# A change to the table of durations from which a layer kernel's order of instructions is computed: transfers by row numbers and accumulations

## The chip, the cores and the metric

The kernel runs on one core of one Trainium2 chip. The metric is the time of one execution on the device in microseconds (us). The kernel before the change takes 2641.74 us, the median of three runs from 2641.53 to 2642.2 us. Five engines work beside each other, each through its own list of instructions: PE (matrix products), DVE and ACT (elementwise work), POOL, and SP. SP issues the large transfers, POOL those whose rows are picked by a list of numbers.

## What is computed

One layer over 2048 tokens of width 1024, in fp32: a mixer (four heads of differential attention, four of mLSTM), cross attention to 256 memory rows, a mixture of 32 experts of which each token takes two, and a last norm. The change shows in the experts and in what follows them:

```
x = x + hybrid_mixer(rms_norm(x, norm_mix_g), ...)
x = x + cross_attention(rms_norm(x, norm_x_g), ...)
x = x + hierarchical_moe(rms_norm(x, norm_ffn_g), ...)
return rms_norm(x, norm_final_g)
# hierarchical_moe: a group (of 4), then the 2 best of its 8 experts for each token;
# the rows of each expert are collected into blocks, and
def run_block(args):
    x_blk, e = args
    return (silu(x_blk @ w1[e]) * (x_blk @ w3[e])) @ w2[e]     # w1, w3: 1024 x 512, w2: 512 x 1024
yb = run_block(...) * buf_w                                    # the token's weight for that expert
out = zeros.at[buf_tok].add(yb)                                # added to the rows of the tokens
```

## The kernel before, in words

No engine's order is written by hand. While the kernel's Python runs, every operation is recorded (`Flow.add`, which is line 521 in nearly every row of the profile, so that groups are told apart by their tiles), and `Flow.run` then works out the order of each engine from a model of the program. `Eng.price` is the table of that model: for each operation the time it holds its engine (`cost`), what passes after that until its result is there (`tail`), and for a transfer the bytes that it moves. `forward` plays the program through with these numbers: whenever an engine is free, it takes the ready operation that is most urgent. All transfers share one model of the transfer engines, `ring`, at 360e3 bytes per us, and land 2.0 us (issued by SP) or 2.7 us (POOL) after their bytes are through. `backward` goes through the finished order from its end and gives each operation the latest time at which it could end; from this comes the urgency for the next round. Of ten rounds that with the shortest modelled span is kept. The order so found is fixed in the program: on the chip each engine goes through its list and waits at an instruction until what it needs is there, and what stands behind it waits too.

The stages in time, by the trace: the mixer up to about 1100 us, cross attention up to 1790, the router and the plan of the experts' blocks up to 1880, the experts up to 2580, and the last norm.

An expert goes as follows. `e_in` gathers its rows with an indirect transfer from POOL (`xg`, two buffers), PE turns them over (matmuls of `ident` with `xg`), ACT and DVE split the result into a high and a low part (`xgT`). Its weights, 6 MB, come in six chunks of 1 MB (`eraw`, issued by SP); each chunk is split into two parts as well (`esp`), in halves: twice an ACT CAST for the high part and twice a DVE TENSOR_TENSOR for the low one. PE multiplies with w1 and w3 (`e_w13`, or `e_two` for experts whose rows stand in two blocks, of 64 rows and of the rest; rows of `esp,xgT` and of `xgT,esp`), ACT and DVE make `hT` of that, PE turns it over where needed (`ident,s`) and multiplies with w2 (`e_out`, rows of `esp,hT`). The results leave PSUM into `ys`, by ACT alone, or for blocks of 64 rows by ACT (`lo`) and DVE. `ys` is one buffer for two blocks. Per block one indirect transfer from POOL adds `ys` to the rows of `x2d` in memory (`x2d<-ys,IDX`, an accumulation); these go strictly one behind another, and the first write into `ys` of the next expert waits until those of the expert before have landed.

The experts go through in a fixed order that ends with number 12, 29, 13, 14, 30 and 31 (numbers by rank; 13 and 14 have two blocks, 30 has one of 104 rows and 31 one of 64). The last two, 30 and 31 (`E[-2]`, `E[-1]`), don't use `e_out`: their results are added in the core and written back. `f_load` then reads all of `x2d` in eight transfers of 1 MB (`fx`, four of them into slots of `esp`). They wait for the last accumulation, that of expert 14. ACT takes the squares (`fsq`), DVE multiplies with the norm, SP writes `out_dram`, and at the very end POOL scatters the rows of experts 30 and 31 into it.

Of the kernel before, what the change touches and what calls it, by code (L numbers as in the profile page):

```python
# [187 lines left out]
class Flow:  # L188
# [133 lines left out]
    def backward(self, order, span):  # L322

        import heapq
        free, wait, can, left, ready = {}, {}, {}, {}, {}

        def offer(o):
            heapq.heappush(wait.setdefault(o.eng, []), (ready[o], -o.stop, -o.seq, o))
        for op in order:
            left[op] = sum(1 for o in op.post if o.pre[op] > -5)  # L330
            ready[op] = 0.0
            free[op.eng] = 0.0
            can.setdefault(op.eng, [])
        for op in order:
            if left[op] == 0:
                offer(op)
        for _ in order:
            best = None
            for e in free:
                w = wait.get(e, [])  # L340
                while w and w[0][0] <= free[e] + 0.02:
                    r, p, i, o = heapq.heappop(w)
                    heapq.heappush(can[e], (p, i, o))
                t = free[e] if can[e] else w[0][0] if w else None
                if t is not None and (best is None or t < best[0]):
                    best = (t, e)
            t, e = best
            op = heapq.heappop(can[e])[2] if can[e] else heapq.heappop(wait[e])[3]
            free[e] = op.late = max(t, ready[op]) + op.cost
            for p, lag in op.pre.items():  # L350
                if lag > -5:
                    ready[p] = max(ready[p], op.late + lag + (p.tail if not p.dma else (2.7 if p.eng == "POOL" else 2.0) + p.dma / 360e3))
                    left[p] -= 1
                    if left[p] == 0:
                        offer(p)
        for op in order:
            op.prio = span - op.late

    def forward(self):
# [66 lines left out]
        ring = 0.0  # L426
# [4 lines left out]
        while len(order) < len(self.ops):  # L431
            best = None
            for e in engines:
                while wait[e] and wait[e][0][0] <= free[e] + 0.02:
                    r, p, i, op = heapq.heappop(wait[e])
# [6 lines left out]
            t, e = best  # L442
            if can[e] and e in self.PATIENT:
                p, i, op = can[e][0]
# [4 lines left out]
            op = heapq.heappop(can[e])[2] if can[e] else heapq.heappop(wait[e])[3]  # L449
# [8 lines left out]
            end = op.start + op.cost + op.tail  # L458
            if op.dma:
                ring = max(ring, t) + op.dma / 360e3  # L460
                end = ring + (2.7 if e == "POOL" else 2.0)
            op.stop = end
            for b in op.banks:
                b.lock = (end + self.LINK, e)
# [21 lines left out]
class Eng:  # L486
# [36 lines left out]
    def price(self, fn, out, ins, kw):  # L523
        if "dma" in fn:
            v = out if isinstance(out, View) else kw["in_"]
            return (1.0 if self.eng == "POOL" else 0.45), 0.0, v.cols * (v.p1 - v.p0) * 4
        n = max([v.cols for v in ins] + [out.cols]) if fn not in ("matmul", "transpose") else out.cols
        psum = any(v.tile.whole for v in ins)
        if self.eng == "PE":
# [1590 lines left out]
```

## Time and profile before

| | us |
|---|---|
| time of a run, median of 3 | 2641.74 |
| the profiled execution: its own time | 2654.76 |
| its span in the trace | 2652.9 |
| PE busy in the span | 2526.1 (95%) |
| DVE busy | 1847.3 (70%) |
| ACT busy | 1440.6 (54%) |

The profiled execution is 13.0 us longer than the median of the runs, and its span 1.9 us shorter than its own time. Times in the sections below are places and lengths in this span, counted from its start. The granted clock over the span is 0.982 of full speed.

### The profile page before, as it was taken

Reading aid. Unit: us, or ns where it says so; the run is one execution under the profiler, and the core shown is the slowest. Engines: PE = TensorE matmul, PEld = TensorE weight load, DVE = VectorE, ACT = ScalarE, POOL = GpSimd, SP = SyncE. Lnnn points to the kernel's source line nnn. Section 1 sums busy time; section 2 is a strip of 40 time slices with the busy share of each in tenths; the row PEclk is TensorE's granted clock in tenths of the full one; section 3 lists DMA queues with packets and bytes.
Section 4 is the critical chain, followed back from the end, with each engine's and each line's share of the span. In section 5 each row is a group of like instructions: output and inputs, shape, how many; then the busy total and the mean of one; then the engine's idle time right before and its main releaser. Section 6 shows DMA issues by size and latency. Waiting matters only on the chain. (4 is left out here: it accounts for less than half of the span.)

```text
span 2652.9 us, 43603 instructions
## 1 busy us (share of the span) xinstructions
PE 2526.1 (95%) x15601; PEld 2241.5 (84%) x15601; DVE 1847.3 (70%) x4586; ACT 1440.6 (54%) x2675; POOL 501.4 (19%) x941
## 2 busy tenths in 40 slices
PE   7999999999999999899999999998999999999981
PEld 7999999899999999897888888886888888887871
DVE  5778767777786779876333335668787878887875
ACT  7766555555565555454212223335676667776753
POOL 2322211121122211101110120111321121121220
PEclk9999999999999999999999999999999999999995
DMA  7435333533253327675222255436999999999986
GB/s 244 157 134 145 108 105 94 147 112 103 94 145 114 109 80 240 200 247 199 88 88 89 79 196 196 144 135 220 311 327 306 326 317 328 316 325 299 302 265 253
DMA packets 207853, 509.92 MB, mean 192 GB/s; under 512 B 22807, under 2 KB 104956, under 8 KB 179986
## 3 DMA queue, kind: packets, MB, share of 16 engines
q1 hardware_dynamic: 181896, 395.16, 43.9%
q0 software_dynamic: 22880, 110.20, 14.0%
q8 instruction: 123, 2.02, 0.3%
q10 hardware_dynamic: 2858, 1.75, 0.2%
q14 instruction: 96, 0.79, 0.1%
HBM read 405.97 MB, written 104.76 MB: 193 GB/s over the span
## 5 line engine op out<-in xcount | busy, mean ns | idle before, releaser
L521 DVE TENSOR_TENSOR esp<-eraw,esp 128x1024 fp32r<-128x1024 f32 x384 | 457.4, 1219 | 109.9 <-ACT esp L521 109.3
L521 ACT CAST esp<-eraw 128x1024 fp32r<-128x1024 f32 x384 | 385.2, 1047 | 161.7 <-PE bank L521 83.7
L521 PE MATMUL bank<-xt,wT 128*128 128x256 f32 x3072 | 449.7, 287 | 5.9 <-DMA xt<-xnT 5.2
L521 PEld LDWEIGHTS bank<-xt,wT 128*128 128x128 f32 x3072 | 406.9, 191 | 15.7 <-DMA xt<-xnT 6.0
L521 PE MATMUL bank<-wR,xt 128*128 128x384 f32 (+1 forms) x1536 | 336.8, 347 | 2.2 <-ACT wR L521 2.2
L521 PEld LDWEIGHTS bank<-wR,xt 128*128 128x128 f32 x1536 | 261.3, 190 | 6.0 <-ACT wR L521 2.8
L521 PE MATMUL bank<-esp,hT 128*128 128x512 f32 (+6 forms) x992 | 248.9, 401 | 5.8 <-DVE hT L521 2.2
L521 PE MATMUL bank<-esp,xgT 128*128 128x512 f32 (+3 forms) x944 | 237.9, 401 | 5.8 <-DVE xgT L521 5.6
L521 PE MATMUL bank<-xgT,esp 128*128 128x256 f32 (+7 forms) x1664 | 241.6, 301 | 1.4 <-DVE s L521 1.1
L521 PEld LDWEIGHTS bank<-xgT,esp 128*128 128x128 f32 x1664 | 231.4, 188 | 4.3 <-DVE s L521 1.2
L521 PEld LDWEIGHTS bank<-esp,hT 128*128 128x128 f32 (+6 forms) x992 | 175.7, 181 | 61.3 <-DVE hT L521 4.3
L521 DVE TENSOR_SCALAR_CACHE_REDUCE P<-bank 128x512 f32<-128x512 f32 (+3 forms) x320 | 191.6, 603 | 30.8 <-PE bank L521 29.6
L521 PEld LDWEIGHTS bank<-esp,xgT 128*128 128x128 f32 (+3 forms) x944 | 167.7, 182 | 52.6 <-DVE xgT L521 3.3
L521 ACT ACTIVATE P<-P,zz 128x128 f32<-128x128 f32 (+15 forms) x128 | 154.1, 1204 | 101.7 <-DVE zz L521 100.2
L521 PE MATMUL bank<-VW,pT 128*128 128x512 f32 x768 | 195.1, 400 | 0.0
L521 PE MATMUL bank<-B,xT 128*128 128x512 f32 x768 | 187.1, 395 | 0.0
L521 PE MATMUL bank<-WO,yT 128*128 128x512 f32 x768 | 185.2, 399 | 0.6 <-issue 0.6
L521 PE MATMUL bank<-V,at 128*128 128x256 f32 x1088 | 180.1, 288 | 0.3
L521 PEld LDWEIGHTS bank<-WO,yT 128*128 128x128 f32 x768 | 143.5, 189 | 34.6 <-issue 0.8
L521 PEld LDWEIGHTS bank<-B,xT 128*128 128x128 f32 x768 | 141.8, 188 | 30.5
L521 PEld LDWEIGHTS bank<-VW,pT 128*128 128x128 f32 x768 | 139.8, 188 | 29.6
L521 PEld LDWEIGHTS bank<-V,at 128*128 128x128 f32 x1088 | 151.7, 189 | 2.7 <-ACT bank L521 0.7
(453 smaller groups left out, 4263.7 us busy)
## 6 DMA issues: line engine op xcount, KB each, us to landing
eraw<-in_w_dram SPq DMA_DIRECT2D x192, 1024.0 KB, 8.2
xt<-xnT POOLq DMA_DIRECT2D x64, 1024.0 KB, 6.1
xr<-in_x_dram SPq DMA_DIRECT2D x32, 512.0 KB, 3.7
xnT<-xt SPq DMA_DIRECT2D x16, 1024.0 KB, 3.9
raw<-in_w_in_dram SPq DMA_DIRECT2D x80, 128.0 KB, 2.8
vod<-vo SPq DMA_DIRECT2D x64, 128.5 KB, 3.1
vi<-vod SPq DMA_DIRECT2D x64, 128.5 KB, 2.5
rt<-in_rope_dram SPq DMA_DIRECT2D x32, 256.0 KB, 2.6
```

Of the source, the lines that this page charges most:

```text
L521: flow.add(self.eng, lambda: real(*[bare(a) for a in args], **{k: bare(v) for k, v in kw.items()}), cost, tail, reads, writes, dma)
```

## The change

In the table, an indirect transfer of 512 columns or more (the gathers of `xg`, the accumulations of `ys`, the write-back and the last scatters) gets a tail of 5.0 us where it had none, and a transfer that accumulates counts 7 bytes an element where it counted 4. `forward` and `backward` add the tail of a transfer, which they left out. Nothing that is computed changes, and no line of the kernel's phases does; the instructions of the mixer and of cross attention keep their prices, but all of the program is ordered anew.

```diff
@@ backward @@
-                    ready[p] = max(ready[p], op.late + lag + (p.tail if not p.dma else (2.7 if p.eng == "POOL" else 2.0) + p.dma / 360e3))
+                    ready[p] = max(ready[p], op.late + lag + p.tail + (0.0 if not p.dma else (2.7 if p.eng == "POOL" else 2.0) + p.dma / 360e3))
@@ forward @@
             if op.dma:
                 ring = max(ring, t) + op.dma / 360e3
-                end = ring + (2.7 if e == "POOL" else 2.0)
+                end = ring + (2.7 if e == "POOL" else 2.0) + op.tail
@@ price @@
         if "dma" in fn:
             v = out if isinstance(out, View) else kw["in_"]
-            return (1.0 if self.eng == "POOL" else 0.45), 0.0, v.cols * (v.p1 - v.p0) * 4
+            rows, add = "indirect" in fn and v.cols >= 512, kw.get("compute_op") is not None
+            return (1.0 if self.eng == "POOL" else 0.45), (5.0 if rows else 0.0), v.cols * (v.p1 - v.p0) * (7 if add else 4)
```

What this does to the order is seen in the rows of the two programs. A row is an instruction in an engine's list; the number behind a tile's name tells the tile of one expert or chunk from that of another and is not the same in both programs.

First place, ACT, in the experts shortly before the end, where expert 27's results (`ys_25880` before the change) and those of its follower 28 (`ys_26012`) are written. Before:

```order
L521 ACTIVATE ys_25880<-bank1_80,WS_20630 104x512
L521 CAST hT_25974<-bank1_80 128x4x104
L521 CAST esp_25995<-eraw_25923 128x1024 x2
L521 ACTIVATE ys_26012<-bank7_86,WS_20630 104x512
L521 CAST esp_26018<-eraw_25967 128x1024 x2
L521 CAST esp_26034<-eraw_25893 128x1024 x2
L521 CAST xgT_26062<-bank6_85 128x4x104
L521 CAST xgT_26062<-bank7_86 128x4x104
L521 CAST esp_26072<-eraw_25987 128x1024 x2
L521 ACTIVATE ys_26012<-bank1_80,WS_20630 104x512
```

The same place of the changed program, where the two are `ys_25809` and `ys_26074` of experts 11 and 27; ahead of these rows stand the two writes of `ys_25809` and two casts of `esp_25881`, and behind them the second write of `ys_26074`:

```order
L521 CAST xgT_25819<-bank5_84 128x4x88
L521 CAST esp_25940<-eraw_25879 128x1024 x2
L521 CAST esp_25954<-eraw_25849 128x1024
L521 CAST hT_25967<-bank5_84 128x4x104
L521 CAST esp_25954<-eraw_25849 128x1024
L521 CAST esp_25985<-eraw_25772 128x1024 x2
L521 CAST esp_26004<-eraw_25927 128x1024 x2
L521 CAST xgT_26019<-bank6_85 128x4x104
L521 CAST esp_26039<-eraw_25976 128x1024 x2
L521 CAST xgT_26019<-bank4_83 128x4x104
L521 ACTIVATE s1_26050<-s1_26050 128x304
L521 ACTIVATE ys_26074<-bank7_86,WS_20630 104x512
```

Between the last write of one expert's `ys` and the first of the next stood two casts of weights before (the same holds between expert 11 and 27); now twelve stand there, and the two writes of one `ys` stand side by side. Over all experts the number of such casts went from between 2 and 16 (in two places 2) to between 6 and 18.

Second place, DVE, around the write of expert 14's first block (`ys_26964` before, `ys_27104` after) and the last chunks of weights. Before:

```order
L521 SCALAR_TENSOR_TENSOR ys_26964<-bank0_79,WS_20630,lo_26952 64x512
L521 TENSOR_TENSOR esp_26943<-eraw_26891,esp_26943 128x1024
L521 SCALAR_TENSOR_TENSOR ys_26964<-bank5_84,WS_20630,lo_26973 64x512
L521 TENSOR_TENSOR esp_26943<-eraw_26891,esp_26943 128x1024
L521 TENSOR_TENSOR xgT_26758<-bank1_80,xgT_26758 128x4x104
L521 TENSOR_TENSOR esp_26991<-eraw_26922,esp_26991 128x1024 x2
L521 TENSOR_TENSOR esp_27011<-eraw_26949,esp_27011 128x1024 x2
L521 TENSOR_TENSOR esp_27026<-eraw_26967,esp_27026 128x1024 x2
L521 TENSOR_TENSOR esp_27053<-eraw_26998,esp_27053 128x1024 x2
L521 TENSOR_TENSOR s1_27045<-s1_27045,bank7_86 104x512
L521 TENSOR_TENSOR esp_27077<-eraw_27022,esp_27077 128x1024 x2
L521 TENSOR_TENSOR xgT_27069<-bank0_79,xgT_27069 128x4x64
```

After (a last chunk, `esp_27115`, follows these rows of before; `esp_27113` is the last chunk of after):

```order
L521 TENSOR_TENSOR esp_27007<-eraw_26934,esp_27007 128x1024 x2
L521 TENSOR_TENSOR esp_27024<-eraw_26956,esp_27024 128x1024 x2
L521 TENSOR_TENSOR esp_27043<-eraw_26976,esp_27043 128x1024 x2
L521 TENSOR_TENSOR esp_27057<-eraw_26996,esp_27057 128x1024 x2
L521 TENSOR_TENSOR s1_27071<-s1_27071,bank5_84 104x512
L521 TENSOR_TENSOR esp_27081<-eraw_27031,esp_27081 128x1024 x2
L521 SCALAR_TENSOR_TENSOR ys_27104<-bank0_79,WS_20630,lo_26986 64x512
L521 TENSOR_TENSOR hT_27099<-bank4_83,hT_27099 128x4x104
L521 TENSOR_TENSOR esp_27113<-eraw_27050,esp_27113 128x1024
L521 SCALAR_TENSOR_TENSOR ys_27104<-bank2_81,WS_20630,lo_27120 64x512
L521 TENSOR_TENSOR esp_27113<-eraw_27050,esp_27113 128x1024
L521 TENSOR_TENSOR lo_27136<-bank3_82,lo_27136 64x512
```

Before, fourteen of these splits of weights stood behind the first write of expert 14's `ys`; now two do. On ACT the writes of `ys_27104` stand likewise behind `hT_27099` of expert 30 and ahead of `esp_27113`.

Third place, PE, from the end of expert 14's product with w2 (`hT2_26857` before, `hT2_26926` after) to experts 30 and 31. Before:

```order
L521 MATMUL bank2_81<-esp_26739,hT2_26857 80x512 x7
L521 MATMUL bank7_86<-esp_26864,xgT_26758 104x512 x3
L521 MATMUL bank6_85<-esp_26832,xgT_26758 104x512 x12
L521 MATMUL bank7_86<-esp_26864,xgT_26758 104x512 x9
L521 MATMUL bank7_86<-esp_26903,xgT_26758 104x512 x12
L521 MATMUL bank0_79<-ident_64,xg_26589 128x64 x4
L521 MATMUL bank5_84<-ident_64,xg_26589 128x64 x4
L521 MATMUL bank4_83<-ind_20610,cap_20611 1x32
L521 MATMUL bank3_82<-ident_64,s1_27045 128x104 x4
L521 MATMUL bank1_80<-esp_26917,xgT_27069 128x512 x8
L521 MATMUL bank6_85<-esp_26943,hT_27092 104x512 x12
L521 MATMUL bank7_86<-esp_26991,hT_27092 104x512 x12
```

Behind these rows before stand 24 matmuls of expert 31 with w1 and w3, its `ident,s`, and its 16 with w2. After:

```order
L521 MATMUL bank6_85<-esp_26771,hT2_26926 80x512 x12
L521 MATMUL bank4_83<-esp_26825,xgT_26863 104x512 x12
L521 MATMUL bank5_84<-esp_26876,xgT_26863 104x512 x12
L521 MATMUL bank3_82<-esp_26919,xgT_26944 128x512 x8
L521 MATMUL bank3_82<-esp_27024,xgT_26944 128x512 x8
L521 MATMUL bank7_86<-esp_27043,xgT_26944 128x512 x3
L521 MATMUL bank4_83<-ident_64,s1_27071 128x104 x4
L521 MATMUL bank7_86<-esp_27043,xgT_26944 128x512 x5
L521 MATMUL bank7_86<-esp_27057,xgT_26944 128x512 x8
L521 MATMUL bank5_84<-esp_26947,hT_27099 104x512 x12
L521 MATMUL bank1_80<-esp_27007,hT_27099 104x512 x12
L521 MATMUL bank6_85<-ident_64,s1_27150 128x64 x4
```

Twelve of expert 30's 36 late matmuls and the eight `ident,xg` of expert 31 moved ahead of expert 14's product; expert 31's products with w1 and w3 moved ahead of expert 30's with w2. In the after program the squares (`fsq`) then stand on ACT with no expert's work among them, where before `lo` and `hT` of expert 31 stood between the first eight.

## Rows read from the trace of the kernel before

**Rows 1.** The stages from the plan on, as windows: from:to, length, busy time (and instructions) of PE, of its weight loads, of DVE, ACT and POOL, then PE's granted clock, the busy share of the transfer engines, GB/s.

```profile
1790.00:1880.00 90.00, 81.36 (x401) 64.36 (x400) 73.62 (x234) 51.61 (x62) 20.81 (x17) 0.92 0.67 229
1880.00:2420.00 540.00, 536.05 (x2984) 455.30 (x2983) 445.22 (x542) 378.98 (x504) 114.92 (x71) 1.00 0.98 323
2420.00:2470.00 50.00, 43.48 (x257) 35.17 (x257) 32.95 (x40) 28.91 (x40) 13.88 (x7) 1.00 0.88 273
2470.00:2580.00 110.00, 102.62 (x584) 83.16 (x583) 88.39 (x117) 73.07 (x103) 28.27 (x11) 0.97 0.89 285
```

**Rows 2.** PE's waits between 2420 and 2470 us: what waited for whom, us in total, times, the longest.

```profile
PE bank L521 <- ACT ys L521: 3.6, 2, 1.9
PE bank L521 <- DMA xg<-xn2d,IDX: 1.8, 1, 1.8
PE bank L521 <- DVE s L521: 1.1, 1, 1.1
```

**Rows 3.** ACT in the order of time, two writes of `ys` in that window: start, length, what, and in brackets how long ACT had been idle before it and what ended that.

```profile
2439.27 0.69 ACT L521 ACTIVATE ys<-bank,WS 104x512 f32<-104x512 f32 x1 [5.07 <-issue]
...
2457.15 0.69 ACT L521 ACTIVATE ys<-bank,WS 104x512 f32<-104x512 f32 x1 [4.98 <-DMA x2d<-ys,IDX]
```

**Rows 4.** Transfers between 1880 and 2605 us by tile, from issue to landing: first the gathers `xg`, then the accumulations from `ys`.

```profile
DMA to landing us min/median/max: 5.0/8.7/13.3
```

```profile
DMA to landing us min/median/max: 5.0/9.9/13.9
```

**Rows 5.** POOL in the order of time: the accumulations of experts 13 (two) and 14 (two), and the last scatter into `out_dram`.

```profile
2535.27 3.65 POOL L521 DMA_INDIRECT x2d<-ys,IDX  x1 [17.23 <-DVE ys L521]
2547.32 2.29 POOL L521 DMA_INDIRECT x2d<-ys,IDX  x1 [8.40 <-ACT esp L521]
2561.02 7.18 POOL L521 DMA_INDIRECT x2d<-ys,IDX  x1 [11.41 <-DVE ys L521]
2575.65 1.44 POOL L521 DMA_INDIRECT x2d<-ys,IDX  x1 [7.45 <-DMA x2d<-ys,IDX]
...
2640.08 0.91 POOL L521 DMA_INDIRECT out_dram<-ys,IO  x1 [3.99 <-DMA out_dram<-ys,IO]
```

**Rows 6.** SP's transfers in the order of time: the last seven chunks of weights, then the first reads of `x2d` for the norm.

```profile
2545.26 22.07 SPq L521 DMA_DIRECT2D eraw<-in_w_dram  x7
2580.74 1.40 SPq L521 DMA_DIRECT2D fx<-x2d  x3
```

**Rows 7.** PE in the order of time from the end of expert 14's product with w2 on.

```profile
2549.88 8.52 PE L521 MATMUL bank<-esp,hT 128*80 128x512 f32 x36
2558.23 1.32 PE L521 MATMUL bank<-esp,xgT 128*104 128x512 f32 x5
2562.43 8.80 PE L521 MATMUL bank<-esp,xgT 128*104 128x512 f32 x31 [2.87 <-DVE xgT L521]
2571.16 0.71 PE L521 MATMUL bank<-ident,xg 64*128 64x64 f32 x8
...
2572.97 0.55 PE L521 MATMUL bank<-ident,s 104*128 104x104 f32 x4 [0.97 <-DVE s L521]
2576.22 3.42 PE L521 MATMUL bank<-esp,xgT 128*128 128x512 f32 x8 [2.70 <-DVE xgT L521]
2579.48 5.69 PE L521 MATMUL bank<-esp,hT 128*104 128x512 f32 x24
2585.01 5.77 PE L521 MATMUL bank<-esp,xgT 128*128 128x512 f32 x24
2598.01 0.69 PE L521 MATMUL bank<-ident,s 64*128 64x64 f32 x4 [7.22 <-DVE s L521]
2599.66 5.51 PE L521 MATMUL bank<-esp,hT 128*128 128x512 f32 x16 [0.96 <-DVE hT L521]
```

**Rows 8.** DVE and then ACT in the order of time where expert 14's `ys` is written, with a half chunk of weights and the `hT` of expert 30 on ACT.

```profile
2558.20 0.74 DVE L521 SCALAR_TENSOR_TENSOR ys<-bank,WS,lo 64x512 f32<-64x512 f32 x1 [4.72 <-DMA x2d<-ys,IDX]
...
2560.00 0.74 DVE L521 SCALAR_TENSOR_TENSOR ys<-bank,WS,lo 64x512 f32<-64x512 f32 x1
```

```profile
2559.04 0.69 ACT L521 ACTIVATE lo<-bank,WH 64x512 f32<-64x512 f32 x1 [5.57 <-DVE ys L521]
2559.75 0.68 ACT L521 ACTIVATE ys<-bank,WS 80x512 f32<-80x512 f32 x1
2560.33 1.03 ACT L521 CAST esp<-eraw 128x1024 fp32r<-128x1024 f32 x1
...
2574.20 0.51 ACT L521 CAST hT<-bank 128x416 fp32r<-128x416 f32 x1
```

**Rows 9.** The last norm, the transfer of its input (issues in the window from 2560 us on: KB each, median us to landing), ACT's first square and what stands ahead of it, DVE's longest wait among the multiplications and its last ones.

```profile
fx<-x2d SPq DMA_DIRECT2D x4, 1024.0 KB, 10.4
```

```profile
2593.20 0.63 ACT L521 ACTIVATE s<-lo 64x512 f32<-64x512 f32 x1 [5.47 <-DVE lo L521]
2593.73 1.04 ACT L521 ACTIVATE fsq<-fx 128x1024 bf16<-128x1024 f32 x1
```

```profile
2613.50 0.17 DVE L521 TENSOR_SCALAR rm_h<-fss 128x4 f32<-128x4 f32 x1 [2.41 <-ACT fsq L521]
...
2627.74 2.48 DVE L521 SCALAR_TENSOR_TENSOR esp<-esp,rm_s,gn 128x1024 f32<-128x1024 f32 x2
```

**Rows 10.** The tiles turned over by PE for the experts (all `ident,xg` matmuls after 1880 us): count, then shortest, median and longest in ns, and the first and last start.

```profile
L521 PE MATMUL bank<-ident,xg x344: 221/253/328, 1884.3 to 2571.6; 64*128 64x64 f32 x56, 128*128 128x128 f32 x24, 120*128 120x120 f32 x24, 112*128 112x112 f32 x24
```

## The prediction

> **What bounds the kernel now.** I read the windows by stage first, since the share over the span hides the ends. From 1880 to 2420 us PE is busy for 536.05 of 540 us and the transfer engines for 0.98 of the time [rows 1]. Two resources are full there at once; an order can gain 4 us at most in this stage, and could lose if it only opened a hole. From 2420 to 2470 PE is busy for 43.48 of 50 us, and from 2470 to 2580 for 102.62 of 110: together 13.9 us of idle PE. So I looked at what ends PE's waits in the first of these holes: ACT's writes of `ys` twice, 3.6 us, then a gather, 1.8, then 1.1, in sum 6.5 [rows 2]. Next, why ACT was late: in the order of time it stands idle for 5.07 and 4.98 us in front of just two writes of `ys` [rows 3]. The second is named as a wait for an accumulation `x2d<-ys` to land. The first is put down to nothing that the profile shows; since it stands at the same place of the next expert, I take it for the same wait. These are the two places where the order has only two casts between the `ys` of two experts. Then the landing times: a gather takes 8.7 us in the median (5.0 to 13.3), an accumulation 9.9 (5.0 to 13.9) [rows 4].
>
> The end is a chain of its own. Expert 14's first accumulation is issued at 2561.02 and its second only at 2575.65, once the first is down [rows 5]; 5.09 us later, at 2580.74, SP issues the reads of `x2d` for the norm [rows 6]. I call that moment T0. From there to the span's end at 2652.9 it is 72.2 us, in which PE bounds nothing. So two numbers make the time: T0, and what follows it.
>
> **The change, part by part.** No instruction is added or removed in the phases; only the order moves. For a block of 104 rows (104 x 4 KB = 426 KB) the old table lets a transfer from POOL land after 2.7 + 1.2 = 3.9 us; the new one says 8.9 for a gather and 2.7 + 2.1 + 5.0 = 9.8 for an accumulation. Against 8.7 and 9.9 in [rows 4] the new numbers fit the median, the old ones are less than half.
>
> In sentences that the rest can do without: the Trainium skill, page "DMA: Bandwidth & Descriptors", section "Anatomy of one DMA — SWDGE (gpsimd) path", gives a fit for a transfer from POOL of about 2.0 us plus its bytes at 436 GB/s, so an estimate of 3.0 us for 426 KB. By it the old table would be right and the new one wait for nothing. The trace disagrees: not even the fastest accumulation was below 5.0 us [rows 4]. By the page's figure expert 14's two accumulations would land in some 2.7 us each, and the sum below would come out 5 us lower.
>
> *Waits of ACT at `ys`.* In the new order at least six casts stand between the `ys` of two experts, twelve at the place that now has two. At about 1.03 us a cast [rows 8], twelve cover 12 us, more than the 9.9 of an accumulation. Six cover only 6, but the old order also has sixes and shows no stall of PE at them: all waits of PE in the 540 us before come to 4 us. I credit all 6.5 us of [rows 2]. Bounds: nothing, if DVE or a late chunk of weights ends the wait instead, and 13.9, all the idle PE of both holes.
>
> *Expert 14's accumulations.* This part speaks against the change. Before, expert 14's product with w2 ends on PE at 2549.88 + 8.52 = 2558.4 [rows 7], and its `ys` follows at once: DVE's second write ends at 2560.74 [rows 8]. The new order puts 12 of expert 30's late matmuls and eight transposes ahead of that product: 12/36 x (1.32 + 8.80) = 3.4, and 0.7 [rows 7]. Behind the product, ACT's writes of `ys` stand in line behind `hT_27099`, which needs expert 30's `ident,s`, and ahead of that PE has 24 matmuls of expert 30 (24/36 x 10.12 = 6.7), 19 of expert 31's 32 (19/32 x (3.42 + 5.77) = 5.5) and the `ident,s` itself (0.55): 12.8. So PE gets there at 2558.4 + 4.1 + 12.8 - 6.5 = 2568.8. From there ACT needs `hT` 0.5, two writes of `ys` 1.4, half a chunk 1.0 and `lo` 0.7, then DVE writes for 0.7 [rows 8]: 4.3, so 2573.1, against 2560.74.
>
> What is gained is the landing. Before, the first accumulation took 14.6 us until the second could go, with weights still streaming to 2567 [rows 5, 6]; the second, with the stream over, took 5.09. In the new order both fall behind the stream. For the first I take 5.5 us, near the floor of 5.0 (upper bound 9.9), and 0.7 for POOL to get the second out (it holds POOL for 1.44 [rows 5]). T0 = 2573.1 + 0.3 + 5.5 + 0.7 + 5.1 = 2584.7, 4.0 later than before. The recovered 6.5 us are in this already: without the late accumulations T0 would be earlier by that. Bounds: PE free of the rest of its holes and 5.0 us, T0 -1; nothing recovered in the first hole and 9.9 us, T0 +11.
>
> *The norm.* Before, the first square waits at 2593.73 for a `lo` of expert 31, with ACT idle for 5.47 us ahead [rows 9], 13.0 us after T0; the reads land 10.4 us after their issue. Now no expert's work stands among the squares. That gives 2.6 us at the start. DVE idles 2.41 us among the multiplications for a square that `lo` held up [rows 9]; of that I take a small part, 0.4, since the reads (1 MB each) then press from behind. In sum -3.0; bounds 0 and -5. PE is no obstacle: after `ident,s` at 2568.8 it has 13/32 x 9.19 + 5.69 + 0.69 + 5.51 = 15.6 us left and ends near 2587 even with 2 us of waits, while the first `fx` lands at T0 + 10.4 = 2595. The old wait of 7.2 us for `s` [rows 7] goes too, and gives nothing, since nobody on the path waits for it.
>
> *The plan.* The first expert's gather is now taken to land 5 us later, and its eight transposes (0.253 us each, 2.0 in sum [rows 10]) stand right ahead of its first product. PE idles for 8.6 us in that stage [rows 1]; partly this moves work out of a hole. +1, bounds 0 and +3.
>
> *Mixer and cross attention.* Prices there are unchanged, the order is another one anyway. PE is nearly full there in both programs' lists; I can't price single rows and take 0, bounds -4 and +4, by what the full stage 1880 to 2420 shows as loss of a good order, 4 us.
>
> Sum: +4.0 - 3.0 + 1 + 0 = +2.0 on the span of 2652.9. The profiled execution's own time, 2654.76, goes to 2656.8; it stands 13.0 above the median, so the median of the runs goes from 2641.74 to about 2643.7. I predict 2643.5. The measurement can tell about 0.2%, 5.3 us, from no change.
>
> **The rivals.**
>
> *Faster.* The stalls go and T0 comes early: PE reaches `ident,s` with no hole left (another 4 us of the 13.9), both accumulations land in 5 us. T0 then is 2580, the norm gives its full 5 us, and the shuffle of the mixer some more: 2641.7 - 1 - 5 - 2 = about 2634. For it: the new prices fit the trace at the median, and the waits in [rows 2, 3] are of just the kind that they forbid. Against it: behind 14's `ys` only two splits of weights are left of fourteen, so what is gained in front is spent at the end.
>
> *Slower.* Expert 14's accumulations still fall into the stream: its last chunk is late, since the old order keeps the transfer engines at 0.89 here [rows 1], the first takes 9.9 us, and the second is behind it. T0 + 9 to + 11, the norm -3, the plan +2: about 2651. It decides from the point where the first accumulation takes over 9 us. For it: before, the same one held the next back for 14.6 us while the last chunks streamed. Against it: in the new order at most the last chunk is under way.
>
> *Nothing moves.* Both resources are full from 1880 to 2420, the hole of 6.5 us only shifts what waits for the last chunks, and T0 follows the stream's end: 2641.7 within 2.
>
> **How the numbers follow.** My sum of parts 0.30, nothing moves 0.12, faster 0.26, slower 0.32. The first two lie within 0.2% mostly: same 0.42. The range leaves out about one in ten on each side: 2630 (beyond the 2634 of the faster case, with the mixer's -4) to 2656 (the slower case with the mixer's +4). Alone, my own sum runs from 2639 to 2648.
>
> **What would show it.** In the profile after: ACT without waits of 5 us ahead of `ys` around 2430 to 2460, and PE's busy time there above 48 of 50 us; expert 14's first accumulation issued at about 2573, landing in 5 to 7 us; the reads `fx` at about 2585; the first square 10 to 11 us after them, and 69 us from `fx` to the end. I am wrong if PE's waits for `ys` stay or turn up elsewhere in the experts, if the accumulations of expert 14 take 9 us and more with the stream over, or if the mixer, where no price changed, moves by more than 4 us.

## The result: 1.1% slower

The changed kernel takes 2672.54 us, the median of four runs (2669.53 to 2676.58), against 2641.97 us of the kernel before. The ratio is 1.0112, with a 95% interval from 1.0099 to 1.0125. I had forecast no change, 2643.5 us, with a range up to 2656; the measured time lies 16.5 us beyond it.

The profiled execution took 2669.53 us, its span is 2667.7. The stages in windows, to be held against [rows 1] (from:to, length, busy time of PE, PEld, DVE, ACT and POOL, granted clock, share of the transfer engines, GB/s):

```profile
1790.00:1880.00 90.00, 80.01 (x392) 62.15 (x391) 70.59 (x219) 51.27 (x63) 21.53 (x17) 0.92 0.71 239
1880.00:2420.00 540.00, 523.35 (x2883) 445.49 (x2882) 427.82 (x512) 362.78 (x479) 113.69 (x67) 0.98 0.95 307
2420.00:2470.00 50.00, 48.63 (x252) 37.23 (x252) 36.85 (x44) 33.09 (x46) 11.75 (x6) 1.00 0.92 296
2470.00:2580.00 110.00, 110.00 (x657) 91.37 (x656) 94.82 (x124) 78.67 (x110) 17.95 (x12) 1.00 0.96 320
```

The holes that I had read between 2420 and 2580 us are gone: PE is busy for 158.63 of 160 us there, against 146.10 before. But the stage ahead, which was full, now loses 16.65 of 540 us where it lost 3.95, and its granted clock falls to 0.98. What PE waits for there, the two largest (what waited for whom, us in total, times, the longest):

```profile
PE bank L521 <- DVE xgT L521: 13.2, 6, 3.6
PE bank L521 <- ACT esp L521: 1.1, 1, 1.1
```

One of these places, on PE, ACT and DVE in the order of time (start, length, what, idle before and what ended it):

```profile
2169.86 0.57 PE L521 MATMUL bank<-ident,xg 120*128 120x120 f32 x4
2171.78 0.63 PE L521 MATMUL bank<-ident,xg 120*128 120x120 f32 x4 [1.34 <-DVE xgT L521]
2174.99 6.70 PE L521 MATMUL bank<-esp,hT 128*112 128x512 f32 x17 [2.58 <-DVE xgT L521]
```

```profile
2167.58 2.00 ACT L521 CAST esp<-eraw 128x1024 fp32r<-128x1024 f32 x2 [1.76 <-DMA eraw<-in_w_dram]
2170.47 0.56 ACT L521 CAST xgT<-bank 128x480 fp32r<-128x480 f32 x1 [0.90 <-PE bank L521]
2170.93 1.99 ACT L521 CAST esp<-eraw 128x1024 fp32r<-128x1024 f32 x2
2172.82 0.56 ACT L521 CAST xgT<-bank 128x480 fp32r<-128x480 f32 x1
```

```profile
2171.06 0.66 DVE L521 TENSOR_TENSOR xgT<-bank,xgT 128x480 fp32r<-128x480 f32 x1
2172.01 2.36 DVE L521 TENSOR_TENSOR esp<-eraw,esp 128x1024 fp32r<-128x1024 f32 x2 [0.29 <-ACT esp L521]
2174.28 0.65 DVE L521 TENSOR_TENSOR xgT<-bank,xgT 128x480 fp32r<-128x480 f32 x1
```

PE's list has both groups of `ident,xg` directly ahead of the product with w2, with nothing between. The second `xgT` stands behind a chunk of weights on ACT (2170.93 to 2172.92) and on DVE (2172.01 to 2174.37). So PE waits until DVE empties the bank. It then takes 6.70 us for 17 matmuls, 394 ns each, where a full stretch takes 236 (43 in 10.14 us, below). The same happens at 2226 and 2390. The windows of 20 us around the three places have the clock at 0.84, 0.83 and 0.83, a mean of the two levels:

```profile
2160.00:2180.00 20.00, 16.07 (x79) 13.19 (x78) 15.39 (x17) 12.84 (x17) 4.14 (x2) 0.84 1.01 319
2220.00:2240.00 20.00, 15.91 (x70) 12.60 (x69) 11.54 (x13) 10.59 (x13) 3.92 (x3) 0.83 0.80 249
2380.00:2400.00 20.00, 14.77 (x77) 11.85 (x75) 10.05 (x11) 7.32 (x9) 2.60 (x2) 0.83 0.97 302
```

The end answers to [rows 5 to 9]. PE, POOL, SP and ACT:

```profile
2574.53 10.14 PE L521 MATMUL bank<-esp,xgT 128*104 128x512 f32 x43
2584.51 0.52 PE L521 MATMUL bank<-ident,s 104*128 104x104 f32 x4
```

```profile
2589.86 2.17 POOL L521 DMA_INDIRECT x2d<-ys,IDX  x1 [24.75 <-DVE ys L521]
2596.17 1.43 POOL L521 DMA_INDIRECT x2d<-ys,IDX  x1 [4.14 <-DMA x2d<-ys,IDX]
```

```profile
1788.11 2.23 SPq L521 DMA_DIRECT2D eraw<-in_w_dram  x4
...
2542.21 36.37 SPq L521 DMA_DIRECT2D eraw<-in_w_dram  x11
2601.22 2.46 SPq L521 DMA_DIRECT2D fx<-x2d  x4
```

```profile
2606.90 1.06 ACT L521 ACTIVATE fsq<-fx 128x1024 bf16<-128x1024 f32 x1 [8.01 <-DMA fx<-x2d]
```

T0, the start of the reads for the norm, is 2601.22 instead of 2580.74, and from there to the end it takes 66.5 us instead of 72.2. That is +20.5 - 5.7 = +14.8, the difference of the two spans. The medians lie 30.6 us apart. The other 15.8 belong to the two profiled executions: that of before took 12.8 us more than its median, that of the changed kernel 3.0 us less. The first experiment is about the 12.8.

How PE fares as a whole shows between the first chunk of weights (the first `eraw` of SP's queue, 1793.24 before and 1788.11 now) and the end of PE's last product. The row of that chunk before, the last product now (before, it ends at 2599.66 + 5.51 = 2605.17 [rows 7]), and the two stretches as windows, first before, then now:

```profile
1793.24 2.13 SPq L521 DMA_DIRECT2D eraw<-in_w_dram  x4
```

```profile
2595.52 5.54 PE L521 MATMUL bank<-esp,hT 128*128 128x512 f32 x16 [0.92 <-DVE hT L521]
```

```profile
1793.24:2605.17 811.93, 777.26 (x4268) 647.87 (x4266) 649.54 (x941) 544.32 (x726) 178.42 (x107) 0.98 0.93 306
1788.11:2601.06 812.95, 783.47 (x4268) 652.37 (x4267) 644.02 (x914) 538.13 (x712) 169.71 (x106) 0.98 0.91 295
```

PE's work takes 1.0 us longer: PE idles 5.2 us less (29.5 for 34.7), and the same matmuls take 6.2 us more. What moved is T0 against that work. It lay 24.4 us ahead of the end of PE's last product, so that the norm began beside PE's last work; now it lies 0.2 us behind it.

### The profile page after: what moved, and what is told of

Its sections match the earlier page's. It is cut to its first block, busy times and chain, and to the rows that moved or that the text cites. A ratio compares the mean times of both kernels' runs of the same rounds, so it can differ in the third digit from the quotient of the medians.

```text
span 2667.7 us, 43596 instructions
## 1 busy us (share of the span) xinstructions
PE 2534.3 (95%) x15601; PEld 2247.1 (84%) x15601; DVE 1849.0 (69%) x4586; ACT 1438.9 (54%) x2675; POOL 492.8 (18%) x941
## 5 line engine op out<-in xcount | busy, mean ns | idle before, releaser
L521 PEld LDWEIGHTS bank<-xt,wT 128*128 128x128 f32 x3072 | 406.7, 191 | 12.6 <-DMA xt<-xnT 3.9
L521 PE MATMUL bank<-esp,hT 128*128 128x512 f32 (+6 forms) x992 | 257.7, 410 | 11.0 <-DVE xgT L521 6.6
```

Of the source, the lines that this page charges most:

```text
L521: flow.add(self.eng, lambda: real(*[bare(a) for a in args], **{k: bare(v) for k, v in kw.items()}), cost, tail, reads, writes, dma)
```

## The experiments

All times of the experiments are medians; each ratio is against runs of the kernel before beside it. For the stage in question I use a length that two rows give: from the first chunk of weights (SP's first `eraw`) to T0. It is 2601.22 - 1788.11 = 813.1 us in the changed kernel and 787.5 before.

**The kernel before, profiled again** (no edit).

> The kernel before, unchanged, with a new profile. Its profiled execution of before took 13.0 us more than the median of its runs, and had 6.5 us of idle PE between 2420 and 2470 us and 7.4 between 2470 and 2580. Theory A (the holes belong to the order): the new profile shows them again at the same two writes of ys, and its time stands as far above the runs as before. Theory B (the holes were what that one execution had too much): the new trace, at about 2642 to 2645 us, has PE at 48 of 50 us and more between 2420 and 2470, and about 10 us less idle PE from 1880 to 2580; then the 6.5 us that the prediction credited were not there to be gained.

Measured: ratio 1.0004 (0.9987 to 1.0020); this profiled execution has a span of 2639.4 us. Its window, PE's first wait in it, and SP's rows:

```profile
2420.00:2470.00 50.00, 44.88 (x273) 36.89 (x273) 34.86 (x44) 29.31 (x41) 12.55 (x8) 1.00 0.93 290
```

```profile
PE bank L521 <- ACT ys L521: 3.5, 2, 1.8
```

```profile
1781.49 2.15 SPq L521 DMA_DIRECT2D eraw<-in_w_dram  x4
...
2541.46 15.82 SPq L521 DMA_DIRECT2D eraw<-in_w_dram  x6
2567.34 1.40 SPq L521 DMA_DIRECT2D fx<-x2d  x3
```

The holes are there again (theory A): they belong to the order. Yet the time does not stand 13 us above the runs. The first profile's excess lies elsewhere: its first chunk came at 1793.2 (the first `eraw` of its SP queue), 11.7 us later than here, with the same program. Everything from there to T0 is as long in both, 787.5 and 785.9 us, and so is the rest, 72.2 and 72.1. Against this profile the changed kernel is 28.3 us longer: 6.6 up to the first chunk (where the same program moves by 11.7 from one execution to another), 27.3 from there to T0, and -5.6 behind it. Split by PE's last product, 2.7 of the 27.3 us are PE's work (810.3 us here) and 24.6 the place of T0 against its end. Split by SP's queue, 12.6 lie behind the last chunk's issue: 2601.22 - (2542.21 + 36.37) = 22.6, against 2567.34 - (2541.46 + 15.82) = 10.1.

**Which of the three numbers.** The change has three parts: the 7 bytes, the tail of the gathers and the tail of the accumulations. They were run in five combinations; the accumulations' tail of 5.0 us by itself is not among them. The line that returns the price, in place of the changed kernel's, for both tails, the bytes alone, the gathers' tail alone, the bytes with the accumulations' tail, and the bytes with the gathers' tail (`...` stands for what stays the same):

```diff
-  (5.0 if rows else 0.0), ... * (7 if add else 4)
+  (5.0 if rows else 0.0), ... * 4
+  0.0, ... * (7 if add else 4)
+  (5.0 if rows and not add else 0.0), ... * 4
+  (5.0 if rows and add else 0.0), ... * (7 if add else 4)
+  (5.0 if rows and not add else 0.0), ... * (7 if add else 4)
```

> The tail of 5.0 us alone, accumulations at 4 bytes. Theory T (the tail makes the loss, by putting the experts' xgT late and side by side): slower than before by most of the 30 us, 2660 to 2675, with waits of PE for DVE xgT of 8 us and more between 1880 and 2450. Theory W (the 7 bytes make it, by filling the modelled ring): about as before, 2640 to 2650. Theory S (any new order loses, since the order of before is the lucky one of many): slower by 5 to 30, with holes at other places than in the changed kernel.

> The 7 bytes alone, no tail. Theory T: within 8 us of before. Theory W: 2660 to 2675, with waits for xgT as in the changed kernel. Theory S: slower by 5 to 30, holes at other places.

> The tail of 5.0 us for transfers by row numbers that don't accumulate (the gathers, the write-back, the last scatters), 4 bytes. If the gathers' tail is what puts the xgT late (theory T in its narrow form): 2655 to 2675 with PE's waits for xgT; expert 14's accumulations as early as before. If it is the accumulations' tail: about as before, 2640 to 2650. Theory S: slower by 5 to 30.

> The 7 bytes and the tail of 5.0 us for accumulations alone; gathers keep no tail. The parts so far: 7 bytes alone 0.9968, gathers' tail alone 1.0067, both tails 1.0054, all three 1.0112. Theory G (the gathers' tail makes the loss, at the plan and in the stream of weights): about 2634 to 2642 here, the plan as long as before (100 us from the first chunk of weights to the 19th, against 103 with the gathers' tail). Theory A (the accumulations' tail makes it, by putting expert 14's accumulations at the end): 2650 to 2665; of the splits of weights 8 stand behind the first write of expert 14's ys (14 before, 2 in the changed kernel), so T0 falls 15 to 18 us behind the last chunk's issue, against 10 to 14 before. Theory S (any other number shuffles the order and costs or gains some 10 us by chance): no order among the four.

> The 7 bytes and the tail of 5.0 us for what does not accumulate; accumulations have no tail. Theory G: 2652 to 2668, the plan 103 us, waits of PE for xgT or s in the stream. Theory A: 2632 to 2644; 18 splits stand behind expert 14's first write, and T0 comes 6 to 10 us after the last chunk. Both parts of the loss standing beside each other would give about 2650 here and in the run before this.

| | ratio (95%) | median, us | first chunk to T0, us | first chunk to the end of PE's last product, us | T0 against that end, us |
|---|---|---|---|---|---|
| before, second profile | 1.0004 (0.9987 to 1.0020) | 2644.2 | 785.9 | 810.3 | -24.4 |
| 7 bytes alone | 0.9968 (0.9955 to 0.9981) | 2633.7 | 775.1 | 796.4 | -21.3 |
| 7 bytes, gathers' tail | 0.9987 (0.9973 to 1.0001) | 2644.1 | 778.4 | 800.5 | -22.1 |
| 7 bytes, accumulations' tail | 1.0089 (1.0068 to 1.0110) | 2669.9 | 814.5 | 812.4 | +2.1 |
| all three: the changed kernel | 1.0112 (1.0099 to 1.0125) | 2672.5 | 813.1 | 813.0 | +0.2 |
| both tails, 4 bytes | 1.0054 (1.0038 to 1.0071) | 2656.0 | 797.6 | 812.6 | -15.0 |
| gathers' tail alone | 1.0067 (1.0042 to 1.0091) | 2659.7 | 799.7 | 824.8 | -25.1 |

SP's rows behind the second and the fourth line, the 7 bytes alone and with the accumulations' tail:

```profile
1789.40 2.14 SPq L521 DMA_DIRECT2D eraw<-in_w_dram  x4
...
2564.50 0.89 SPq L521 DMA_DIRECT2D fx<-x2d  x2
```

```profile
1788.37 2.21 SPq L521 DMA_DIRECT2D eraw<-in_w_dram  x4
...
2602.88 2.26 SPq L521 DMA_DIRECT2D fx<-x2d  x4
```

The 7 bytes alone make the kernel faster, which none of the theories had. Adding the gathers' tail to them costs 0.2%, adding the accumulations' tail 1.2% and 39.4 us on the way to T0: 15.9 of them in PE's work, 23.5 in the place of T0 against its end. With the latter, PE's waits between 1880 and 2420 us are those of the changed kernel, and without it there are hardly any. First the 7 bytes with the accumulations' tail, then without:

```profile
PE bank L521 <- DVE xgT L521: 13.7, 7, 3.5
```

```profile
PE bank L521 <- DVE esp L521: 0.6, 1, 0.6
PE bank L521 <- ACT esp L521: 0.2, 1, 0.2
```

So where the 7 bytes stand, the accumulations' tail makes the loss (theory A of the two pairs), and a larger one than that theory's 2650 to 2665. Theory W (the bytes lose) falls. With 4 bytes it is otherwise: the accumulations' tail costs nothing on top of the gathers' (1.0054 against 1.0067). The loss there comes with the gathers' tail and lies in PE's work, 824.8 us, while T0 keeps its place ahead of PE's end.

**Chance or size.** The whole change with other tails, and the 7 bytes with smaller tails of accumulations:

```diff
-  (5.0 if rows else 0.0)
+  (4.8 if rows else 0.0)
+  (6.0 if rows else 0.0)
+  (2.0 if rows and add else 0.0)
+  (3.5 if rows and add else 0.0)
```

> The whole change with a tail of 4.8 us in place of 5.0. If the loss follows from the size of the prices, 2668 to 2676 as with 5.0. If the order that comes out is chance (theory S), it lies 8 us or more from 2672; the order says 12 splits behind expert 14's first write against 2, which by the chain from there alone would give about 8 to 10 us less: 2660 to 2666.

> The whole change with a tail of 6.0 us. If the loss grows with the price: 2674 to 2684. If it is chance (theory S): anywhere from 2635 to 2680, off the line through 0 us (2634), 4.8 and 5.0. 5 splits stand behind expert 14's first write: T0 18 to 22 us behind the last chunk.

> The 7 bytes and a tail of 2.0 us for accumulations alone. So far, with 7 bytes: no tail 2634, accumulations' tail of 5.0 us 2670. Theory C (the planner holds the accumulations, which go one behind another through one ys, for the bound, and turns the order towards them; a chip on which they take 9.9 us is not bound by them): the loss sets in where two accumulations and what stands between them pass an expert's period of some 23 us, so 2.0 us on top of the 7 bytes cost part of it, 2643 to 2660. Theory L (each us of tail pushes the last accumulations later, in proportion): 2634 + 2/5 of 36 = 2648. Theory S (chance): anything from 2630 to 2675. 10 splits stand behind expert 14's first write, 16 without tail, 8 with 5.0 us.

> 7 bytes and an accumulations' tail of 3.5 us, between 2.0 (0.9969) and 5.0 (1.0089). Theory C: a step, since the loss begins where the chain becomes the planner's bound: near one of the two, 2634 to 2642 or 2660 to 2672, or on the step. In proportion (theory L from 2.0 on): 1.0029, about 2651.

Measured, with 7 bytes and no gathers' tail: 0.9968 at 0 us, 0.9969 (0.9954 to 0.9984) at 2.0, 1.0034 (1.0014 to 1.0053) at 3.5, 1.0089 at 5.0; to T0 it takes 775.1, 782.6, 799.4 and 814.5 us. With both tails: 1.0069 (1.0047 to 1.0092) at 4.8, 1.0112 at 5.0, 1.0120 (1.0098 to 1.0141) at 6.0. Seven orders of their own stand in line with the size of the price, so chance (theory S) does not make the trend. But chance is in it: at 4.8 us the ratio is 0.4% lower than at 5.0 (8.3 us between the medians, about the 8 that I had named as its sign), more than 0.2 us of price explains. In its profile the way to T0 is no shorter for it (817.5 us against 813.1); the first chunk comes 9.3 us earlier. So two orders of nearly the same prices can differ by 0.4%, and it is the 1.2% between 0 and 5.0 us that stands clear of this. Nor is there the step of theory C at 3.5: the loss is nothing up to 2.0 us, where both theories expected one, and then grows with the tail. At 2.0 us T0 already lies only 8.2 us ahead of PE's end; nothing is lost by it, since PE's work takes just 790.9 us and 67.0 us follow T0 instead of 73.7. SP's rows at 2.0 us:

```profile
1786.98 2.14 SPq L521 DMA_DIRECT2D eraw<-in_w_dram  x4
...
2569.61 2.08 SPq L521 DMA_DIRECT2D fx<-x2d  x4
```

**Tail, or lateness in all.** Accumulations with 3.0 us and 4 bytes, and with 10 bytes and no tail:

```diff
-  (5.0 if rows else 0.0), ... * (7 if add else 4)
+  (3.0 if rows and add else 0.0), ... * 4
+  0.0, ... * (10 if add else 4)
```

> A tail of 3.0 us for accumulations alone, at 4 bytes an element. What counts in theory C is how late the planner lets an accumulation land in all, behind the chunks that are queued ahead of it: the 7 bytes delay all of the queue, the 3.0 us only the accumulation, to about the same moment. Theory C: no loss, 2630 to 2648. Theory L: 2642 + 3/5 of 36 = 2664. If the gain of the 7 bytes is that they let the chunks of weights land later too (theory E), it is absent here: 2638 to 2648; if it is the later accumulation, it is here as well: 2630 to 2638.

> Accumulations at 10 bytes, no tail at all. If an accumulation that is thought too slow makes the loss in whatever way it is written down (theory C): 2650 to 2675, T0 15 us and more behind the last chunk. If only the tail does it, since it comes on top of the queue (theory L): 2630 to 2645, T0 5 to 8 us behind the last chunk; 14 splits stand behind expert 14's first write, as before the change.

Measured: 0.9987 (0.9963 to 1.0010) and 1.0043 (1.0028 to 1.0057). A tail of 3.0 us on 4 bytes costs nothing; 10 bytes without any tail lose as well. It is not the tail as such. Whether the gain of the 7 bytes is there with the 3.0 us can't be told, since the two intervals overlap. The bytes also delay the chunks queued behind an accumulation, which I did not try by itself. How late the planner lets an accumulation land can be read from its own play of the program (`op.stop` less `op.start` in the round that `forward` keeps; numbers of the host program, none of the chip), as the median of the 44 accumulations:

| order | planner: landing, us | ratio |
|---|---|---|
| before | 7.1 | 1.0004 |
| 4 bytes, gathers' tail | 7.4 | 1.0067 |
| the same without the plan's gather (last experiment) | 7.4 | 1.0054 |
| 4 bytes, 3.0 us | 10.1 | 0.9987 |
| 7 bytes, gathers' tail | 10.9 | 0.9987 |
| 7 bytes | 11.1 | 0.9968 |
| 7 bytes, 2.0 us | 11.6 | 0.9969 |
| 10 bytes | 12.3 | 1.0043 |
| 4 bytes, both tails | 12.4 | 1.0054 |
| 7 bytes, 3.5 us | 12.5 | 1.0034 |
| 7 bytes, 5.0 us | 13.2 | 1.0089 |
| both tails of 4.8 us | 13.2 | 1.0069 |
| the changed kernel | 13.3 | 1.0112 |
| both tails of 6.0 us | 13.9 | 1.0120 |
| the changed kernel, tail out of the chain (next experiment) | 13.7 | 1.0027 |
| 7 bytes, 5.0 us, tail out of the chain (next experiment) | 14.5 | 1.0030 |

The trace puts the landing at 9.9 us in the median before [rows 4], and in the changed kernel at 9.1:

```profile
DMA to landing us min/median/max: 4.9/9.1/12.8
```

The orders between 10 and 11.6 us are the good ones; beyond 12 the loss sets in. But this median does not decide alone: the gathers' tail loses at 7.4 us, and the two orders that believe in landings of 13.7 and 14.5 us lose the least of those beyond 12. Nor is the order nearest to the trace the fastest: that is the one with 10.1 us, and 11.1 and 11.6 gave the fastest. In the planner a transfer stands in one queue behind the chunks of weights, 1 MB / 360e3 = 2.9 us each, and the table's numbers come on top of that. I had left the queue out when I found that 9.8 us fit.

**The chain in the planner.** The changed kernel, and the 7 bytes with the accumulations' tail alone, both with one more edit: in the planner's play an accumulation waits only until 4.9 us before the one ahead of it is down, and no longer until 0.13 us behind that (`LINK`). So the tail of 5.0 us is out of the chain; the bytes and the queue are still in it.

```diff
                     if last[0] is not None:
-                        self.link(op, last[0], self.LINK)
+                        self.link(op, last[0], -4.9 if <both accumulate> else self.LINK)
```

> The whole change, but in the planner's play an accumulation no longer waits for the landing of the accumulation ahead of it (it still does on the chip). Each keeps its 7 bytes and 5.0 us towards those who read x2d or write ys next. Theory C: the chain is what the planner turned its order towards, so the larger part of the loss goes: 2645 to 2660. If the tail harms as the latency of a single accumulation: 2666 to 2678, as in the changed kernel.

> As e11 (an accumulation does not wait for the one ahead of it in the planner's play), with the 7 bytes and the accumulations' tail of 5.0 us but no tail for gathers: e4 with the chain cut. Theory C with the plan's share: e4 gave 1.0089, e11 1.0027; the loss goes but for 0 to 6 us, 2636 to 2652, and the plan takes 99 to 100.5 us from the first chunk of weights to the 19th. Against it: 2655 to 2672, if the tail harms as the latency of single accumulations and e11 was a lucky order.

Measured: 1.0027 (1.0010 to 1.0043) instead of 1.0112, and 1.0030 (1.0009 to 1.0052) instead of 1.0089. To T0 it takes 798.1 instead of 813.1 us, and 791.9 instead of 814.5. The waits of PE for `xgT` between 1880 and 2580 us are 5.6 and 2.5 us in sum, instead of 13.2 and 15.1. Against the same prices without the accumulations' tail (0.9987 and 0.9968), 0.4 of 1.25% is left in the first and 0.6 of 1.2% in the second. So half to two thirds of the loss goes when the tail leaves the chain. What comes back is mostly PE's work: 798.1 us instead of 813.0, and 798.2 instead of 812.4. T0 stays at PE's end in the first and lies 6.2 us ahead of it in the second. The rest may come from the lateness of each accumulation towards those who wait for it, or from what is still in the chain; no run parts these.

**The gathers' tail where it stands alone.** As in the third run, but with no tail for the plan's gather of the first expert:

```diff
-  (5.0 if rows and not add else 0.0)
+  (5.0 if rows and not add and not v.tile.kw['name'].startswith('xg0') else 0.0)
```

> e3 (gathers' tail alone, 1.0067) but for the plan's one gather, that of the first expert, which has no tail. If that gather makes the 3 to 4 us by which the plan is longer in all runs that have the tail (102.0 to 105.8 us against 99 to 100.5): plan 99 to 101 us here, time 3 to 4 us under e3, 2652 to 2658. If the rest of e3's loss (10 to 14 us, in the experts) is tied to the gathers, it stays; if it was the chance of one order, it goes: 2640 to 2648.

Measured: 1.0054 (1.0028 to 1.0079), 804.1 us to T0. The plan is as long as with that tail, 104.0 us from the first chunk's issue in the trace to the nineteenth's (103.9 in the third run), against 100.4 in the second profile of before. So that one gather is not what makes the plan longer, and its loss in the experts stays too. I have no cause for it: the same tail costs 0.2% beside the 7 bytes and 0.7% without them.

## Why the prediction was wrong, point by point

- **"The new numbers fit the median, the old ones are less than half."** A wrong reading, though no term of the sum hangs on it; it spoke for the rival "faster". I compared the table's numbers with landings in the trace, 9.8 against 9.9 us. The planner adds the queue of weights to them. Before the change its landings had a median of 7.1 us, a little short; the 7 bytes alone bring 11.1; with the tail it is 13.3, a third longer than the trace's 9.9. What I took for a better table was one that counts the same delay twice.
- **The waits at `ys`, 6.5 us.** Only 3.6 of them were waits at `ys` [rows 2]; I credited the 1.8 for a gather and the 1.1 for an `s` with them. They were the order's, as the second profile shows, and the change removed them there: 48.63 of 50 us. Right for that place.
- **The price of the new order in the full stage.** This is the step of the sum that failed. I wrote that an order "could lose if it only opened a hole" there, and gave that no term; the 0 ± 4 us stand for the mixer and cross attention. So the 6.5 us were taken as a net gain, and with the holes at the end gone but for 2 us PE was to be through near 2587, 18 us sooner than the 2605.2 of before. It was through at 2601.06, and counted from the first chunk it took 1.0 us longer than before. What I forecast as gain came: from 2420 us to its last product PE idles 2.8 us instead of 22.1, 19.3 less. What had no price took it all: 12.7 us more of idle PE in the full stage, where PE waits 13.2 us for `xgT`, 1.4 more ahead of it, and matmuls that take 6.2 us longer, with a clock that falls at three places. In sum that is 20.3. I had seen in the new order only that six casts or more stand between two `ys`, not where the transposes now stand. From 1880 us on the trace has five places where both groups stand directly ahead of a product with w2; before it had none. The place alone is not enough, since the order with the 7 bytes alone has five such places too and no wait behind them; at the three that wait, an `xgT` of the pair stands behind a chunk of weights on ACT and DVE. A row "nothing waits here now" in a full stage says nothing about what another order does there.
- **Expert 14's accumulations, T0 + 4.0.** It was +20.5. PE was to reach `ident,s` at 2568.8 and got there at 2585.0, its end in the row of 2584.51: that is the step above, not this one. That the order puts expert 14's accumulations behind nearly all of PE's work I had seen, and I had priced that work at 4.1 + 12.8 us; what I took off for it, a PE that is through sooner, did not come. From there on the working held: 16.2 us from the end of `ident,s` to T0 against my 15.9 (2568.8 to 2584.7), and the second accumulation 6.3 us behind the first against 6.2.
- **The norm, -3.0.** It gained 5.7 us, a little beyond my bound of -5. The first square starts at 2606.90, 5.7 us after T0, with ACT waiting for the read alone; before it was 13.0. I had the reads land after 10.4 us [rows 9], a median over issues, and so gave the start 2.6 us of gain. The trace of before had the quickest of the four reads down after 5.0 us (`fx` by its tile, below). In the changed kernel the same view gives 10.2 to 10.5 us for all four, which does not fit a square that starts after 5.7; how long the first read takes there is open but for that bound.

```profile
DMA to landing us min/median/max: 5.0/8.3/11.6
```

- **The plan, +1 (0 to +3).** 103.3 us against 100.4 in the second profile of before, +2.9 and inside the bounds, and against 99.6 in the first, +3.7 and a little beyond them. The reason that I gave, the first expert's gather, is not borne out.
- **Mixer and cross attention, 0 ± 4.** 1788.1 up to the first chunk, between the two profiles of the unchanged kernel (1781.5 and 1793.2). Nothing can be told.
- **The 13.0 us between profile and median.** I subtracted them as if they lay outside the change. That was sound: 11.7 of them lay ahead of the experts.
- **The rival "slower"** named the right place and the wrong reason: expert 14's first accumulation took 6.3 us until the next, not over 9. It came late since everything ahead of it was late.
- **The fit of the Trainium skill** (page "DMA: Bandwidth & Descriptors", section "Anatomy of one DMA — SWDGE (gpsimd) path"), about 2.0 us plus the bytes at 436 GB/s, does not give the landings here either: no accumulation of the changed kernel was down in less than 4.9 us.

## What to carry to other kernels

A measured duration belongs into a planner's table only after taking off what the planner adds by itself: compare what the planner believes, queue and all, with the trace, not the entry with the trace. That alone does not give the fastest order, as the table of landings shows. The price of a latency did its harm here where it repeats in a chain: half to two thirds of the loss went when the tail left the chain. That the planner then turns its urgency to the chain and takes it from the engine that bounds the kernel is my explanation; I did not read it from the planner. The 7 bytes alone (0.9968) were worth more than bytes and tail together (1.0112).

When all of a program is ordered anew, look in the new order for two things: stretches that lost their cover on the bounding engine, in the full stages above all, and what still runs beside that engine's last work. Here T0 went from 24.4 us ahead of PE's end to 0.2 us behind it.

## What the runs showed of the hardware that I had not expected

Behind its three holes PE runs slowly for a while. PE in the order of time behind the second and the third (the first is shown above):

```profile
2226.19 0.60 PE L521 MATMUL bank<-ident,xg 112*128 112x112 f32 x4 [1.74 <-DVE xgT L521]
2229.15 7.38 PE L521 MATMUL bank<-esp,hT 128*112 128x512 f32 x19 [2.35 <-DVE xgT L521]
...
2393.28 0.96 PE L521 MATMUL bank<-ident,xg 104*128 104x104 f32 x4 [3.56 <-DVE xgT L521]
2395.90 4.41 PE L521 MATMUL bank<-esp,hT 128*96 128x512 f32 x12 [1.66 <-DVE xgT L521]
```

That is 388 and 368 ns a matmul, and 394 behind the first, against 237 for the same kind of matmul in a full stretch of the kernel before (36 in 8.52 us [rows 7]). What PE did at each place ahead of that was to wait twice for `xgT`, 3.9 to 5.2 us in sum. The granted clock of the windows, 0.84, 0.83 and 0.83, is a mean of the two levels, 2.4 and 1.2 GHz. The loss is (394 - 237) x 17 + (388 - 237) x 19 + (368 - 237) x 12 = 7.1 us, about half of the 13.2 us of the waits themselves, and comes on top of them; I had priced holes by their waits alone. In the kernel before, the four waits of up to 1.9 us between 2420 and 2470 us [rows 2] left the clock of their window at 1.00 [rows 1].

And the same program reached its first chunk of weights at 1781.5 us in one execution and at 1793.2 in another, so that one profile can stand 0.4% off in a stage that has nothing to do with the change. What makes the difference is open; the two were profiled in separate series of runs.
